# Pooled projections by seven block products, trailing sums by a scan

## The chip, the cores and the metric

The kernel runs on one core of a Trainium2 chip. The metric is the device time of one execution in microseconds (us); a time given for a kernel is the median over several executions. The core has five engines that run their own instruction queues in order and meet through semaphores: TensorE (PE, with its weight loads listed as PEld), VectorE (DVE), ScalarE (ACT), GpSimd (POOL) and SyncE (SP), which here issues DMA transfers. Matrix products read operands in SBUF, the on-chip memory of 128 partitions, and leave results in eight PSUM banks of 128 x 512 fp32.

## The reference

The model is a trunk of two residual layers on an input of 512 tokens by 1024 channels. Each layer computes x + RMSNorm(mixer(RMSNorm(x))). The first layer's mixer has mLSTM heads and stick-breaking attention and is not touched. The second layer's mixer is the one that the change concerns:

```python
def odd_layer(x, pre_g, post_g, w_in, pool_w, pool_scale, w_out):
    h = rmsnorm(x, pre_g)
    u = h @ w_in                                # (512 x 1024) @ (1024 x 4096)
    p, z = u[..., :C_WIDTH], u[..., C_WIDTH:]   # 2048 columns each
    pooled = multiscale_pool(p.reshape(Bn, S, C_GROUPS, C_GROUP_DIM))   # 4 groups of 512
    mixed = jnp.einsum('bsgc,gce->bsge', pooled, pool_w)                # one 512 x 512 map a group
    mixed = mixed.reshape(Bn, S, C_WIDTH) * pool_scale
    y = (mixed * jax.nn.silu(z)) @ w_out
    return x + rmsnorm(y, post_g)
```

`multiscale_pool` takes, for each group, the mean of the last 2, 4, 8 or 16 tokens (fewer at the start) and subtracts the token itself.

## The kernel before

All data are fp32 and every large product is made of three matmuls in a reduced-precision fp32 type. The helper `split` (lines 70 to 72) cuts an operand into a high part (a ScalarE copy, line 71) and the rest (a VectorE subtraction, line 72); `mm3` (lines 93 to 97) then adds high x high, high x low and low x high into one PSUM bank. A weight is loaded by one DMA on the SP queue into one of two 1 MB buffers (`load`, line 83), split by `halves` into one of four pairs of buffers `wh`/`wl`, and used as the stationary operand. Activations lie transposed, channels on partitions and the 512 tokens along the free axis: `hTh` and `hTl` hold the normalised input's two parts.

The second layer loops over the four groups (line 734). For each group it does the following.

- **The pooled columns p**: four chunks of 128 channels, taken as two pairs of 256 columns. Group one does them in two token halves. Groups two to four call `project2` (line 751): for each pair one load, two splits of 128 x 1024, and for each chunk 24 matmuls of 512 tokens (8 channel blocks x 3 terms) into a bank `pj`, copied out by ScalarE (line 752).
- **Pooling** (lines 753 to 775): each chunk's tile has 16 zero columns ahead of its 512 tokens. Window sums are made by doubling: 1, 2, 3 or 4 adds of a shifted copy on VectorE (line 762), each into a new tile whose leading zeros POOL sets (line 761). POOL corrects the first tokens, whose windows are shorter (lines 767 and 768), VectorE scales the sum and subtracts the token (line 769), and `split` makes the operand `pph`, `ppl`.
- **The gate columns z**: two pairs of 256 columns. In groups two to four they are made by `strassen2` (line 688), with SiLU on the way out.
- **The map** `mx`: one load and two splits of the group's 512 x 512 map `pw`, then four tiles of 12 matmuls of 512 tokens into the two banks `ac`. VectorE multiplies each tile with the scale and the gate (line 797).

`strassen2` computes a product of 256 columns by 512 tokens as a 2 x 2 block product (channel halves, column halves, token halves) with seven block products instead of eight. The token-side sums are made once, after group one, by `hidden_sums`. For each pair VectorE makes four sums of weight blocks, four split sets follow (`first` to `fourth`, the last one half as wide), and the products go in this order, each of 12 matmuls of 256 tokens:

```python
product(pa, first, 0, "11", True, True);  A.activation(t1, pa, AF.Copy)
product(pb, first, 4, "21", True, True);  V.tensor_tensor(dsts[0][:, :256], pb, t1, op=ALU.add)
product(pa, second, 0, "n2", False, True); A.activation(t2, pa, AF.Copy)
product(pe, second, 4, "d1", True, True); A.activation(t5, pe, AF.Copy)
product(pa, third, 0, "d3", False, True)
V.scalar_tensor_tensor(dsts[1][:, 256:], pa, -1.0, t5, op0=ALU.mult, op1=ALU.subtract)
product(pe, third, 4, "22", False, True); V.tensor_tensor(dsts[0][:, 256:], pe, t2, op=ALU.add)
product(pa, fourth, 0, "t4", False, True)
```

The bank `pa` is one of the two `pj`, `pb` is `xa` and `pe` is `xb`, of which there is one each. `pa` goes on accumulating after it has been read, so each later product into it must come after the read.

The order of the instructions on each engine is fixed when the kernel is built. The framework takes the program as written, estimates each instruction's time, and places each one where its engine would be free and its operands ready. On the chip the order stays as placed, so an engine whose next instruction waits does nothing else, even where another would be ready. Among the matmuls of one group's map stand some of the next group's pooled matmuls.

Of the kernel before, what the change touches and what calls it, by code (L numbers as in the profile page):

```python
# [5 lines left out]
F32 = mybir.dt.float32  # L6
F32R = mybir.dt.float32r
AF = mybir.ActivationFunctionType
ALU = mybir.AluOpType
# [4 lines left out]
P = 128  # L14
S = 512
# [21 lines left out]
def body(nc, tc, x, pre_g, post_g, w_in, conv, b_i, b_f, hn_g, w_out, w_in_c, pool_w,  # L37
         pool_scale, w_out_c, out):
    V, A, G, T = nc.vector, nc.scalar, nc.gpsimd, nc.tensor
# [4 lines left out]
    with base as base, psum as psum, dram as dram:  # L44
# [141 lines left out]
        def col_load(src, name):  # L186

            w = load(lambda t: [(nc.sync, t, src)], 8, 256, name)
            return [lambda i=i: halves(w[:, :, i * P:i * P + P], f"{name}_{i}") for i in range(2)]
# [6 lines left out]
        def project2(src, name):  # L196
            for i, w in enumerate(col_load(src, name)):
                ps = pj(f"ps_{name}_{i}")
                col_proj(w(), ps)
                yield ps  # L200

        with tc.tile_pool(name="att", bufs=1) as at:
# [25 lines left out]
            for tt in range(NB):  # L228
                prenorm(xt0[tt], xs0[tt % 2], tt, gain0, f"p0{tt}", 1 if tt else 2)
                if tt == 0:  # L230
                    for i in range(2):
                        if i:
                            nc.sync.dma_start(xt0[1], xr[:, 1])
                        w = load(lambda t: [(nc.sync, t[:, 2 * j:2 * j + 2],
                                             w_in[0, 512 * i + 256 * j:512 * i + 256 * j + 256,
                                                  VB:VB + 512]) for j in range(2)], 4, 512, f"v01{i}")
# [352 lines left out]
            for h in range(HA):  # L589
# [7 lines left out]
                for s in range(NB):  # L597
                    t = bc[:, ROW[s]:ROW[s] + P]
# [28 lines left out]
        with tc.tile_pool(name="odd", bufs=1) as od:  # L627
# [60 lines left out]
            def strassen2(src, name, dsts, silu=False):  # L688

                w = load(lambda t: [(nc.sync, t, src)], 8, 256, name)  # L690
                a11, a12, a21, a22 = (w[:, 4 * k:4 * k + 4, m * P:m * P + P]
                                      for m in range(2) for k in range(2))
                sums = [ws(f"ws{i}_{name}") for i in range(2)]
                s1, s2, s3, s4 = sums[0][:, 4:], sums[0][:, :4], sums[1][:, :4], sums[1][:, 4:]
                first = halves(w[:, :, :P], f"{name}_a")
                V.tensor_tensor(s1, a21, a22, op=ALU.add)
                V.tensor_tensor(s2, s1, a11, op=ALU.add)
                second = halves(sums[0], f"{name}_b")
                V.tensor_tensor(s3, a11, a21, op=ALU.add)
                V.tensor_tensor(s4, a12, s2, op=ALU.add)  # L700
                third = halves(sums[1], f"{name}_c")
                fourth = halves(a22, f"{name}_d")

                def product(ps, wt, k0, b, start, stop):
                    (wh, wl), (bh, bl) = wt, hs[b]
                    for k in range(4):
                        mm3(ps, (wh[:, k0 + k], wl[:, k0 + k]), (bh[:, k], bl[:, k]),
                            start and k == 0, stop and k == 3, skip_group_check=True)

                def part(i): return od.tile([P, 256], F32, tag="part", bufs=4, name=f"pt{i}_{name}")  # L710

                pa, pb, pe = (f(f"ps{n}_{name}")[:, :256] for f, n in ((pj, "a"), (xa, "b"), (xb, "e")))
                t1, t2, t5 = part(1), part(2), part(5)
                product(pa, first, 0, "11", True, True)
                A.activation(t1, pa, AF.Copy)
                product(pb, first, 4, "21", True, True)
                V.tensor_tensor(dsts[0][:, :256], pb, t1, op=ALU.add)
                product(pa, second, 0, "n2", False, True)
                A.activation(t2, pa, AF.Copy)
                product(pe, second, 4, "d1", True, True)  # L720
                A.activation(t5, pe, AF.Copy)
                product(pa, third, 0, "d3", False, True)
                V.scalar_tensor_tensor(dsts[1][:, 256:], pa, -1.0, t5, op0=ALU.mult, op1=ALU.subtract)
                product(pe, third, 4, "22", False, True)
                V.tensor_tensor(dsts[0][:, 256:], pe, t2, op=ALU.add)
                product(pa, fourth, 0, "t4", False, True)
                if silu:
                    act(dsts[0], dsts[0], AF.Silu)
                    act(dsts[1][:, 256:], dsts[1][:, 256:], AF.Silu)
                    act(dsts[1][:, :256], pa, AF.Silu, scale=-1.0)  # L730
                else:
                    A.activation(dsts[1][:, :256], pa, AF.Copy, scale=-1.0)

            for g, w in enumerate(WINDOWS):
                pooled = []
                cur4 = []
                for j in range(4):
                    c = 4 * g + j
                    cur = od.tile([P, 16 + S], F32, tag="win", bufs=6, name=f"p_{c}")
                    G.memset(cur[:, :16], 0.0)  # L740
                    cur4.append(cur)
                wsrc = [w_in_c[0, :, 512 * g + 256 * i:512 * g + 256 * i + 256] for i in range(2)]
                if g == 0:
                    wj = [t() for i in range(2) for t in col_load(wsrc[i], f"p{g}{i}")]
                    for j, n0 in ((j, n0) for n0 in (0, 256) for j in range(4)):
                        ps = pj(f"ps_p{4 * g + j}_{n0}")
                        col_proj(wj[j], ps, n0, n0 + 256)
                        A.activation(cur4[j][:, 16 + n0:16 + n0 + 256], ps[:, n0:n0 + 256], AF.Copy)  # L748
                else:
                    for i in range(2):  # L750
                        for j, ps in enumerate(project2(wsrc[i], f"p{g}{i}")):
                            A.activation(cur4[2 * i + j][:, 16:], ps, AF.Copy)
                for j in range(4):
                    c = 4 * g + j
                    cur = cur4[j]
                    p32 = cur[:, 16:]
                    sh = 1
                    while sh < w:
                        nx = od.tile([P, 16 + S], F32, tag="win", bufs=6, name=f"p_{c}_{sh}")
                        if 2 * sh < w:  # L760
                            G.memset(nx[:, :16], 0.0)
                        V.tensor_tensor(nx[:, 16:], cur[:, 16:], cur[:, 16 - sh:16 + S - sh],  # L762
                                        op=ALU.add)
                        cur, sh = nx, 2 * sh
                    sm = cur[:, 16:]
                    e = w - 1
                    G.tensor_tensor(sm[:, :e], sm[:, :e], invc[:, :e], op=ALU.mult)  # L767
                    G.tensor_tensor(sm[:, :e], sm[:, :e], p32[:, :e], op=ALU.subtract)
                    V.scalar_tensor_tensor(sm[:, e:], sm[:, e:], 1.0 / w, p32[:, e:], op0=ALU.mult,
                                           op1=ALU.subtract)  # L770
                    ph = od.tile([P, S], F32R, tag="phi", bufs=5, name=f"pph{c}")
                    pl = od.tile([P, S], F32R, tag="plo", bufs=5, name=f"ppl{c}")
                    split(sm, ph, pl)
                    pooled.append((ph, pl))
                sz = []
                for i in range(2):
                    zsrc = w_in_c[0, :, 2048 + 512 * g + 256 * i:2304 + 512 * g + 256 * i]
                    pair = [od.tile([P, S], F32, tag="sz", bufs=4, name=f"sz{4 * g + 2 * i + j}")
                            for j in range(2)]
                    if g == 0:  # L780
                        for j, ps in enumerate(project2(zsrc, f"z{g}{i}")):
                            act(pair[j], ps, AF.Silu)
                    else:
                        strassen2(zsrc, f"z{g}{i}", pair, True)
                    sz.extend(pair)
                if g == 0:
                    hidden_sums()
                w4 = load(lambda t: [(nc.sync, t, pool_w[0, g])], 4, 512, f"pw{g}")
                pw = [halves(w4[:, 2 * i:2 * i + 2], f"pw{g}{i}") for i in range(2)]
                for e in range(4):  # L790
                    c = 4 * g + e
                    ps = ac(f"mx{c}")
                    for k in range(4):
                        wh, wl = pw[k // 2]
                        mm3(ps, (wh[:, k % 2, e * P:e * P + P], wl[:, k % 2, e * P:e * P + P]),
                            pooled[k], k == 0, k == 3)
                    V.scalar_tensor_tensor(y32[:, c], ps, psc(c), sz[e], op0=ALU.mult, op1=ALU.mult)
# [44 lines left out]
```

## Time and profile before

| | before |
|---|---|
| median of 3 runs | 914.85 us (914.61 to 915.66) |
| profiled execution | 914.12 us, span 912.2 us |
| busy PE, PEld | 897.8 us, 764.9 us |
| busy DVE, ACT, POOL | 570.6, 485.6, 77.3 us |
| mean granted TensorE clock | 0.995 |
| HBM read | 96.02 MB |

The profiled execution is one run with the profiler on; its span goes from the first to the last instruction, and its own time is 1.9 us longer. A row of a group of instructions gives the line of the kernel (often a helper's line), the engine and the operation, the tiles written and read, the shape and the count; then the busy time, the mean duration of one in ns, and the idle time of the engine before them with what ended it. In a row of the timeline the first two numbers are the start and the duration in us, and square brackets hold the idle time before the instruction. A matmul's row lasts until its results are out, so rows of consecutive matmuls overlap.

### The profile page before, as it was taken

Reading aid. Unit: us, or ns where it says so; the run is one execution under the profiler, and the core shown is the slowest. Engines: PE = TensorE matmul, PEld = TensorE weight load, DVE = VectorE, ACT = ScalarE, POOL = GpSimd, SP = SyncE. Lnnn points to the kernel's source line nnn. Section 1 sums busy time; section 2 is a strip of 40 time slices with the busy share of each in tenths; the row PEclk is TensorE's granted clock in tenths of the full one; section 3 lists DMA queues with packets and bytes.
Section 4 is the critical chain, followed back from the end, with each engine's and each line's share of the span. In section 5 each row is a group of like instructions: output and inputs, shape, how many; then the busy total and the mean of one; then the engine's idle time right before and its main releaser. Section 6 shows DMA issues by size and latency. Waiting matters only on the chain.

```text
span 912.2 us, 12027 instructions
## 1 busy us (share of the span) xinstructions
PE 897.8 (98%) x4669; PEld 764.9 (84%) x4669; DVE 570.6 (63%) x847; ACT 485.6 (53%) x814; POOL 77.3 (8%) x221
## 2 busy tenths in 40 slices
PE   7999999999999999999999999999999999999996
PEld 6788889889988888898898887898889898988885
DVE  5435546567876685664775738578484867957442
ACT  6426676766668464564565527574244343455331
POOL 2001101001101201001001000005020110200000
PEclk8999999999999999999999999999999999999999
DMA  8231322222222421333312456623223233146321
GB/s 301 79 107 47 94 71 69 70 70 60 81 93 87 133 93 66 113 94 127 98 49 91 139 185 210 205 93 119 66 92 117 71 127 105 51 160 231 132 96 46
DMA packets 67128, 98.91 MB, mean 108 GB/s; under 512 B 2848, under 2 KB 54136, under 8 KB 67072
## 3 DMA queue, kind: packets, MB, share of 16 engines
q1 hardware_dynamic: 65888, 98.08, 32.7%
q8 instruction: 36, 0.59, 0.2%
q10 hardware_dynamic: 1184, 0.08, 0.1%
q14 instruction: 20, 0.16, 0.1%
HBM read 96.02 MB, written 2.13 MB: 108 GB/s over the span
## 4 chain that ended last, share of the span: by engine, by line
PE 96%; DVE 1%; ACT 1%; DMA 1%; issue 0%; SPq 0%; DVEq 0%; POOL 0%; POOLq 0%; ACTq 0%
PE op L540 10%; PE oq L540 10%; PE ps_qa L97 3%; PE ps_qa L95 3%; PE ps_qa L96 3%; PE ps_p L95 3%; PE ps_p L97 3%; PE ps_p L96 3%; PE psv_va L95 2%; PE psv_va L97 2%; PE psv_va L96 2%; PE ps_zb L95 2%; PE mx L96 2%; PE mx L97 2%; PE mx L95 2%; PE ps_oa L96 2%
## 5 line engine op out<-in xcount | busy, mean ns | idle before, releaser
L95 PE MATMUL ps_p<-hTh,wh_p 128*128 128x512 f32 (+1 forms) x160 | 55.8, 350 | 0.4 <-ACT p L748 0.4
L96 PE MATMUL ps_p<-hTl,wh_p 128*128 128x512 f32 (+1 forms) x160 | 55.9, 350 | 0.2 <-DVE hTl L72 0.2
L97 PE MATMUL ps_p<-hTh,wl_p 128*128 128x512 f32 (+1 forms) x160 | 55.7, 348 | 0.0
L97 PE MATMUL ps_qa<-hTh,wl_qa 128*128 128x512 f32 x128 | 50.3, 393 | 0.0
L95 PE MATMUL ps_qa<-hTh,wh_qa 128*128 128x512 f32 x128 | 50.2, 393 | 0.0
L96 PE MATMUL ps_qa<-hTl,wh_qa 128*128 128x512 f32 x128 | 50.2, 392 | 0.0
L72 DVE TENSOR_TENSOR wl_wo_e<-w_wo_e,wh_wo_e 128x1024 fp32r<-128x1024 f32 x28 | 34.3, 1232 | 23.3 <-ACT wh_wo_e L71 23.2
L71 ACT ACTIVATE wh_wo_e<-w_wo_e 128x1024 fp32r<-128x1024 f32 x28 | 29.4, 1058 | 29.0 <-DMA w_wo_e<-in_w_out_ab 12.3
L71 ACT ACTIVATE wh_p<-w_p 128x1024 fp32r<-128x1024 f32 x16 | 16.9, 1058 | 51.1 <-issue 31.9
L540 PE MATMUL op<-wh_wo_e,yl_e 128*128 128x512 f32 x120 | 39.1, 396 | 0.0
L540 PE MATMUL op<-wl_wo_e,yh_e 128*128 128x512 f32 x120 | 39.1, 396 | 0.0
L540 PE MATMUL op<-wh_wo_e,yh_e 128*128 128x512 f32 x120 | 37.8, 395 | 0.0
L67 ACT ACT_TABLE_LOAD x28 | 35.9, 1283 | 1.3 <-PEq L827 0.8
L97 PE MATMUL psv_va<-wh_va,hTl 128*128 128x256 f32 x128 | 36.1, 282 | 0.0
L95 PE MATMUL psv_va<-wh_va,hTh 128*128 128x256 f32 x128 | 36.1, 282 | 0.0
L96 PE MATMUL psv_va<-wl_va,hTh 128*128 128x256 f32 x128 | 36.1, 282 | 0.0
L320 DVE SCALAR_TENSOR_TENSOR cv<-u,vecs,cv 128x511 f32<-128x511 f32 (+2 forms) x48 | 35.4, 748 | 0.4
L95 PEld LDWEIGHTS ps_p<-hTh,wh_p 128*128 128x128 f32 x160 | 30.1, 189 | 4.7 <-ACT p L748 0.6
L96 PEld LDWEIGHTS ps_p<-hTl,wh_p 128*128 128x128 f32 x160 | 30.2, 189 | 4.3 <-DVE hTl L72 0.4
L97 PEld LDWEIGHTS ps_p<-hTh,wl_p 128*128 128x128 f32 x160 | 30.2, 189 | 4.1
L72 DVE TENSOR_TENSOR wl_wo_o<-w_wo_o,wh_wo_o 128x1024 fp32r<-128x1024 f32 x20 | 24.3, 1223 | 12.5 <-ACT wh_wo_o L71 12.4
L767 POOL TENSOR_TENSOR p<-p,invc 128x1 f32<-128x1 f32 (+3 forms) x16 | 18.4, 1151 | 157.8 <-DVE p L762 157.7
(379 smaller groups left out, 2826.9 us busy)
## 6 DMA issues: line engine op xcount, KB each, us to landing
w_wo_e<-in_w_out_ab SPq DMA_DIRECT2D x14, 1024.0 KB, 4.8
w_wo_o<-in_w_out_c SPq DMA_DIRECT2D x12, 1024.0 KB, 4.8
w_qa<-in_w_in_ab SPq DMA_DIRECT2D x8, 1024.0 KB, 4.9
w_p<-in_w_in_c SPq DMA_DIRECT2D x8, 1024.0 KB, 5.3
w_z<-in_w_in_c SPq DMA_DIRECT2D x8, 1024.0 KB, 5.3
w_qb<-in_w_in_ab SPq DMA_DIRECT2D x4, 1024.0 KB
w_kb<-in_w_in_ab SPq DMA_DIRECT2D x4, 1024.0 KB, 5.2
w_zb<-in_w_in_ab SPq DMA_DIRECT2D x4, 1024.0 KB, 5.1
```

Source lines behind the costliest of these rows:

```text
L67: link(A.preload_act_table_set(TABLE[func]))
L71: A.activation(hi, src, AF.Copy)
L72: V.tensor_tensor(lo, src, hi.bitcast(F32), op=ALU.subtract)
L95: T.matmul(dst, lhsT=ah, rhs=bh, start=first, stop=False, **kw)
L96: T.matmul(dst, lhsT=ah, rhs=bl, start=False, stop=False, **kw)
L97: T.matmul(dst, lhsT=al, rhs=bh, start=False, stop=last, **kw)
L320: V.scalar_tensor_tensor(acc[:, j:], u[:, :S - j], cw(3 - j, c), acc[:, j:], op0=ALU.mult, op1=ALU.add)
L540: T.matmul(ps[a][n], lhsT=l[:, ta], rhs=r[:, 0, n * 512:n * 512 + 512], start=(first and l is yh and r is wh), stop=(last and l is yl))
L767: G.tensor_tensor(sm[:, :e], sm[:, :e], invc[:, :e], op=ALU.mult)
```

## The change

Two things change in the loop over the groups. In groups two to four the two pooled pairs are made by `strassen2` in place of `project2`; its results are written straight into the chunks' tiles behind the 16 zero columns. The window sums of 4, 8 and 16 are made by one instruction for each chunk, a scan along the tokens: the running sum takes in the new token and gives up the one that leaves the window, `w` columns back, where the leading zeros stand in for tokens before the first. The window of 2 keeps its single add. Tiles for intermediate sums, and the clears of their leading columns, are gone. The gate pairs, the map, the loads and the output projection are written as before.

```diff
                 else:
                     for i in range(2):
-                        for j, ps in enumerate(project2(wsrc[i], f"p{g}{i}")):
-                            A.activation(cur4[2 * i + j][:, 16:], ps, AF.Copy)
+                        strassen2(wsrc[i], f"p{g}{i}", [t[:, 16:] for t in cur4[2 * i:2 * i + 2]])
                 for j in range(4):
                     c = 4 * g + j
                     cur = cur4[j]
                     p32 = cur[:, 16:]
-                    sh = 1
-                    while sh < w:
-                        nx = od.tile([P, 16 + S], F32, tag="win", bufs=6, name=f"p_{c}_{sh}")
-                        if 2 * sh < w:
-                            G.memset(nx[:, :16], 0.0)
-                        V.tensor_tensor(nx[:, 16:], cur[:, 16:], cur[:, 16 - sh:16 + S - sh],
-                                        op=ALU.add)
-                        cur, sh = nx, 2 * sh
-                    sm = cur[:, 16:]
+                    sm = od.tile([P, 16 + S], F32, tag="win", bufs=6, name=f"s_{c}")[:, 16:]
+                    if w == 2:
+                        V.tensor_tensor(sm, p32, cur[:, 15:15 + S], op=ALU.add)
+                    else:
+                        V.tensor_tensor_scan(sm, p32, cur[:, 16 - w:16 + S - w], 0.0, ALU.add,
+                                             ALU.subtract)
```

## The prediction

> **What bounds the kernel now.** I first read the page: its busy shares and the chain that ended last.
>
> ```profile
> span 912.2 us, 12027 instructions
> ...
> PE 897.8 (98%) x4669; PEld 764.9 (84%) x4669; DVE 570.6 (63%) x847; ACT 485.6 (53%) x814; POOL 77.3 (8%) x221
> ...
> PE 96%; DVE 1%; ACT 1%; DMA 1%; issue 0%; SPq 0%; DVEq 0%; POOL 0%; POOLq 0%; ACTq 0%
> ```
>
> TensorE (PE) is 96% of the chain, so time leaves only where TensorE's own work shrinks. Shares are averages, so I next asked for the busy time in the three stretches that hold groups two, three and four (windows of 4, 8, 16), each from one group's map matmuls `mx` to the next's. The columns are the length, then the busy time and records of PE, PEld, DVE, ACT and POOL.
>
> ```profile
> 650.00:702.70 52.70, 52.70 (x311) 46.54 (x310) 34.50 (x48) 22.35 (x34) 5.11 (x17) 1.00 0.28 89
> 702.70:756.25 53.55, 53.55 (x314) 47.26 (x313) 38.11 (x54) 21.84 (x34) 6.64 (x20) 1.00 0.31 99
> 756.25:809.60 53.35, 53.35 (x313) 46.98 (x313) 40.65 (x58) 22.68 (x35) 6.51 (x18) 1.00 0.33 109
> ```
>
> PE is busy for the whole of all three at a granted clock of 1.00. VectorE (DVE) is the next fullest, at 65 to 76%, and it is the engine onto which the change puts work.
>
> A busy PE may still hide small gaps, because one matmul lasts longer than the distance to the next start. So I take start-to-start distances. The first fence is one of the three groups of matmuls (one for each of the lines 95, 96 and 97, all of 8) in one 128-column half of a pooled pair. The second has the busy time of the gate pairs' stretch, which already uses seven products, from its first matmul to the first `mx`, and of four pooled halves.
>
> ```profile
> L95 PE MATMUL ps_p<-hTh,wh_p 128*128 128x512 f32 x8 | 3.1, 389 | 0.0
> ```
>
> ```profile
> 677.48:694.24 16.76, 16.76 (x142) 16.76 (x141) 10.90 (x16) 11.19 (x19) 1.59 (x10) 1.00 0.37 120
> ...
> 719.74:725.21 5.47, 5.47 (x26) 4.50 (x25) 4.42 (x7) 1.83 (x3) 0.24 (x2) 1.00 0.06 22
> 725.33:730.80 5.47, 5.47 (x26) 4.51 (x25) 5.26 (x9) 2.09 (x3) 1.85 (x5) 1.00 0.00 0
> 666.29:671.89 5.60, 5.60 (x27) 4.51 (x25) 4.59 (x7) 1.32 (x2) 0.11 (x1) 1.00 0.01 2
> 772.98:778.45 5.47, 5.47 (x26) 4.51 (x25) 4.93 (x8) 1.83 (x3) 1.19 (x5) 1.00 0.10 34
> ```
>
> A half is 24 matmuls (three groups of 8) in 5.47 or 5.60 us, or 0.228 to 0.233 us each. The gate stretch has 142 records, one of them running in from before: 16.76 / 141 = 0.1189 us for a 256-column matmul, with the weight loads busy throughout (16.76 of 16.76). So the seven-product form runs at the matmul pace and its weight loads don't lengthen it.
>
> **The change part by part.**
>
> *Fewer matmul columns.* A pooled pair was two halves: 2 x 5.50 (mean of the four rows) = 11.00 us, between 10.94 and 11.20. It becomes 7 products x 4 blocks x 3 terms = 84 matmuls of 256: 84 x 0.1189 = 9.99 us. A pair saves 1.01 us (0.95 to 1.21), and six pairs in three groups save **6.1 us** (5.7 to 7.3). This lies wholly on the path.
>
> *More preparation.* The durations are those of the gate pairs' same instructions, and of the old pooled split and adds, from 640 to 812 us:
>
> ```profile
> L762 DVE TENSOR_TENSOR p<-p 128x512 f32<-128x512 f32 x36 | 24.6, 686 | 1.3 <-POOL p L768 0.4
> L72 DVE TENSOR_TENSOR wl_p<-w_p,wh_p 128x1024 fp32r<-128x1024 f32 x12 | 14.7, 1221 | 11.4 <-ACT wh_p L71 11.2
> ...
> L769 DVE SCALAR_TENSOR_TENSOR p<-p,p 128x509 f32<-128x509 f32 (+2 forms) x12 | 8.2, 682 | 0.3
> ...
> L72 DVE TENSOR_TENSOR wl_z_d<-w_z,wh_z_d 128x512 fp32r<-128x512 f32 x6 | 4.1, 687 | 0.1
> ...
> L723 DVE SCALAR_TENSOR_TENSOR sz<-psa_z,pt_z 128x256 f32<-128x256 f32 x6 | 2.5, 418 | 0.0
> ```
>
> On VectorE a pair had two wide splits (2 x 1.22 = 2.44 us). It gets three wide splits and a half one (3 x 1.22 + 0.69 = 4.35), four weight sums (4 x 0.69 = 2.74, as the adds of the same shape) and three output sums (3 x 0.42 = 1.25): 8.34, which is 5.9 more per pair and 11.8 per group.
>
> *The running sum.* The 36 adds go: 8, 12 and 16 in the three groups, or 5.5, 8.2 and 11.0 us. Each of the 12 chunks gets one scan of 512 columns instead; group one keeps its add. The trace before has no scan. Its lower bound is an add, 0.686 us. A two-operation instruction (L769) costs the same 0.682, so the second operation itself is free; what is new is that each column needs the finished sum of the column before. The costliest elementwise row, in the mLSTM heads, gives the upper bound:
>
> ```profile
> L412 DVE RECIPROCAL dd<-dd 128x512 f32<-128x512 f32 x4 | 13.4, 3354 | 2.1 <-ACT dd L68 2.1
> ```
>
> The range is 0.69 to 3.35 us. I take 1.22, the row of 1024 columns, as if each column passed twice: of the three rows it is the nearest to a column that does one more round. A group's VectorE work then changes by 11.8 + 4.9 less its adds: 34.5 becomes 45.7, 38.1 becomes 46.6, 40.65 becomes 46.4 us, against TensorE stretches of 50.7, 51.5 and 51.3 (each 2 x 1.01 shorter). It is hidden by TensorE's own matmuls and costs nothing, but at 90% instead of 71% the cover is thin; without it I price it under the third rival. [...]
>
> POOL loses 24 clears of intermediate tiles, all off the chain.
>
> *What waits anew.* The split weights rotate through four buffers. A pooled pair used two, now it uses four, so its third and fourth sets inherit the buffers of the previous group's map weights and wait for the end of `mx`. The trace before shows this wait for its second pair:
>
> ```profile
> 712.44 1.22 DVE L72 TENSOR_TENSOR wl_p<-w_p,wh_p 128x1024 fp32r<-128x1024 f32 x1
> 712.50 0.39 PE L97 MATMUL mx<-pph,wl_pw 128*128 128x512 f32 x1
> ...
> 713.03 1.06 ACT L71 ACTIVATE wh_p<-w_p 128x1024 fp32r<-128x1024 f32 x1 [0.63 <-PE mx L97]
> ```
>
> The third set would be whole at 712.44 + 1.22 = 713.66, and the last `mx` gives way at 712.50 + 0.23 = 712.73: 0.9 us are to be covered. The pair's first two sets hold 48 matmuls, 48 x 0.1189 = 5.7 us. Of pooled matmuls TensorE used some as filler between the `mx` tiles:
>
> ```profile
> 702.71 0.39 PE L95 MATMUL ps_p<-hTh,wh_p 128*128 128x512 f32 x1
> ...
> 707.13 0.40 PE L95 MATMUL mx<-pph,wh_pw 128*128 128x512 f32 x1
> ```
>
> If these 4.4 us of filler stay, 1.3 us remain after `mx`, against the 0.9 needed: covered, barely. If not, up to one ScalarE and one VectorE pass (1.06 + 1.22 = 2.3 us) opens per group. Queued behind the waiting ScalarE copy are the PSUM copies of the same pair. ScalarE itself has room: a pair gives it eight instructions where it had four, none longer than this 1.06, so at most 4.2 us more a pair, or 8.5 a group on 22 of 53 us.
>
> The 1 MB weight loads keep their number and queue (SP). Their buffer frees at a pair's last split, so the first gate load now waits for the first pair's fourth set, whose copy can't start before 713.03. By the row below it lands some 5 us after that split, near 721; it is needed two pairs (20 us) after `mx`, near 732, so nothing is late.
>
> ```profile
> w_z<-in_w_in_c SPq DMA_DIRECT2D x6, 1024.0 KB, 5.3
> ```
>
> *Hand-overs between pairs.* The gate pairs follow each other with hardly a gap; the worst is in group four:
>
> ```profile
> 789.85 0.28 PE L96 MATMUL psb_z<-hTl,wh_z_a 128*128 128x256 f32 x1
> 790.05 0.38 PE L97 MATMUL psa_z<-hTh,wl_z_a 128*128 128x256 f32 x1
> ```
>
> There 0.20 us lie between starts where 0.12 is usual. A group gets two more seven-product pairs, and I charge 0.1 us, rounded up from this 0.08, for each: **0.6 us** (0 to 7, the bound being the 2.3 us per group).
>
> *The sum.* The profiled execution took 914.12 us, its span 912.2 and 1.9 around it. 914.12 - 6.1 + 0.6 = 908.6. The median of the runs is 914.85, 0.73 above, so the same change gives **909.3** there.
>
> **The rivals.**
>
> *Hand-overs eat the gain (914.1).* Inside a pair the last product accumulates into a bank that VectorE must first have read (L723). The cover is one product, 12 x 0.1189 = 1.43 us. If a scan (1.22) and a half split (0.69) stand ahead of that read (0.42), 2.33 - 1.43 = 0.9 us is lost in each of six pairs, 5.4 of the 6.1. For it: VectorE serves its queue in order and is 90% full. Against it stands a stretch of group four with two pooled halves and most of the gate pairs:
>
> ```profile
> 774.20:797.90 23.70, 23.70 (x160) 21.76 (x159) 23.10 (x35) 11.51 (x20) 5.34 (x14) 1.00 0.14 46
> ```
>
> VectorE was 97% busy, and TensorE showed no idle time beside the short gap above.
>
> *POOL is locked out (911.4).* POOL's edge correction waits while VectorE works back to back:
>
> ```profile
> 619.85 7.45 POOL L767 TENSOR_TENSOR p<-p,invc 128x1 f32<-128x1 f32 x1 [71.84 <-DVE p L762]
> ...
> 793.08 0.64 POOL L767 TENSOR_TENSOR p<-p,invc 128x15 f32<-128x15 f32 x1 [5.37 <-DVE p L762]
> 795.70 0.69 DVE L72 TENSOR_TENSOR ppl<-p,pph 128x512 fp32r<-128x512 f32 x1
> 801.10 0.39 PE L95 MATMUL mx<-pph,wh_pw 128*128 128x512 f32 x1
> ```
>
> One column took 7.45 us instead of 0.64. Were the last chunk of group four held so, 6.8 us more, it would pass its 4.7 us of slack (796.39 to 801.10) by 2.1 us. Against it: VectorE's own next step waits for POOL and so stops. [...]
>
> *VectorE becomes the bound: slower (919.4).* Here the mechanism is the scan alone. The group is VectorE-bound at its old length when 38.1 + 11.8 - 8.2 + 4X = 53.55, so X = 2.96 us; the other two groups give 2.98. At the upper bound of 3.35 the groups last 54.2, 55.1 and 54.9, together 4.6 us more than now. For it only the reciprocal's row speaks; against it, an add and subtract in one pass cost 0.68. [...]
>
> **How the numbers follow.** Forecast 0.60 at 909.3 (own range 907.5 to 911.5: 914.85 - 7.3 without a stall, and 914.85 - 5.7 with one of 2.3). POOL 0.05 at 911.4. Hand-overs 0.24 around 914.1, spread over faster 0.06, same 0.13 and slower 0.05. Scan 0.11 at 919.4. A measurement here tells 0.2%, about 1.8 us, from no change. Faster: 0.60 + 0.05 + 0.06 = 0.71; same 0.13; slower 0.05 + 0.11 = 0.16. The range runs from 907.0, the forecast's own low end less half the 1.05 us by which the three runs differ, to 915.5, which leaves out the scan's case and the dear end of the hand-overs.
>
> **What would show it.** Right: the three groups shorten to about 51.5 us with PE busy throughout; 84 matmuls of 256 per pooled pair at 0.119; the scan's row near 1.2 us; VectorE near 46 us per group. Wrong: PE idle before the pooled products of the third set or before the last product of a pair, released by VectorE or ScalarE; `mx` waiting for `ppl`; a scan row above 2.9 us; a 256-column pitch above 0.131 (11.00 / 84), at which the pairs save nothing.

## The result and the profile after

The changed kernel takes **908.97 us** (median of 6 runs, 907.92 to 910.40) against 914.66 us for the kernel before on the same chip (6 runs). The ratio is 0.9939, with a 95% interval of 0.9928 to 0.9949. A second set of five runs on another occasion gave 908.57 us and 0.9938 (0.9925 to 0.9950). The prediction was 909.3 us, within 907.0 to 915.5. The profiled execution took 910.17 us, 1.2 above the median.

The page of the changed kernel, with its busy shares and the chain that ended last:

```profile
span 908.5 us, 12491 instructions
...
PE 893.6 (98%) x4885; PEld 771.9 (85%) x4885; DVE 590.8 (65%) x877; ACT 497.9 (55%) x838; POOL 82.4 (9%) x197
...
PE 93%; DVE 3%; DMA 2%; ACT 1%; issue 1%; SPq 0%; DVEq 0%; POOL 0%; ACTq 0%; POOLq 0%
```

TensorE has 216 more matmuls and is still 98% busy, but VectorE and a DMA now hold 5% of the chain; before, they held 2%. The busy times of the three groups, each cut at its first pooled matmul and the last at the first of the output projection, show where. First the kernel before, then the changed one:

```profile
649.40:702.71 53.31, 53.31 (x314) 47.05 (x313) 34.91 (x48) 22.35 (x34) 5.11 (x17) 1.00 0.29 92
702.71:756.09 53.38, 53.38 (x314) 47.10 (x313) 37.94 (x54) 21.84 (x34) 6.64 (x20) 1.00 0.31 99
756.09:809.51 53.42, 53.42 (x314) 47.06 (x312) 40.77 (x58) 22.59 (x35) 6.51 (x18) 1.00 0.33 109
```

```profile
650.61:701.72 51.11, 51.11 (x385) 48.93 (x384) 41.05 (x58) 26.09 (x42) 7.70 (x12) 1.00 0.32 104
701.72:754.76 53.04, 51.78 (x385) 49.13 (x384) 45.23 (x63) 25.90 (x43) 7.66 (x12) 1.00 0.32 100
754.76:806.05 51.29, 51.29 (x385) 48.99 (x384) 42.81 (x59) 25.95 (x42) 7.99 (x8) 1.00 0.34 114
```

Groups two and four shortened by 2.2 and 2.1 us with PE busy throughout, group three by 0.3. Group three shows 51.78 us of busy PE in 53.04: it lost 1.3 us to waits, and more if the short gaps hidden under a matmul's own duration are counted. The view of who waited for whom on PE, from 615 to 812 us, names the two longest:

```profile
PE psa_z L97 <- DVE wl_z_a L72: 0.7, 1, 0.7
PE psa_z L95 <- DVE sz L723: 0.5, 1, 0.5
```

The first is followed in the timelines of VectorE and PE:

```profile
717.54 0.69 DVE L696 TENSOR_TENSOR ws_z<-w_z 128x512 f32<-128x512 f32 x1 [2.13 <-DMA w_z<-in_w_in_c]
...
721.07 1.21 DVE L760 TENSOR_TENSOR_SCAN s<-p 128x512 f32<-128x512 f32 x1
722.21 1.20 DVE L72 TENSOR_TENSOR wl_p_c<-ws_p,wh_p_c 128x1024 fp32r<-128x1024 f32 x1
723.32 0.68 DVE L72 TENSOR_TENSOR wl_p_d<-w_p,wh_p_d 128x512 fp32r<-128x512 f32 x1
723.93 0.68 DVE L765 SCALAR_TENSOR_TENSOR s<-s,p 128x505 f32<-128x505 f32 x1
724.53 1.21 DVE L72 TENSOR_TENSOR wl_z_a<-w_z,wh_z_a 128x1024 fp32r<-128x1024 f32 x1
```

```profile
724.79 0.27 PE L97 MATMUL psa_p<-d3h,wl_p_c 128*128 128x256 f32 x1
725.80 0.39 PE L97 MATMUL psa_z<-hTh,wl_z_a 128*128 128x256 f32 x1 [0.73 <-DVE wl_z_a L72]
```

VectorE first waited 2.13 us for the gate weights to land. Then it worked without a break, with a scan, a scaling and two other splits ahead of the split `wl_z_a`, which ended at 725.74; PE, which would have gone on at 724.91, started at 725.80. A scan's row is in the groups of lines, from 640 to 812 us:

```profile
L760 DVE TENSOR_TENSOR_SCAN s<-p 128x512 f32<-128x512 f32 x12 | 14.6, 1219 | 0.0
```

### The profile page after: what moved, and what is told of

It is laid out like the page before. It is cut to its first block, busy times and chain, and to the rows that moved or that the text cites. A ratio compares the mean times of both kernels' runs of the same rounds, so it can differ in the third digit from the quotient of the medians.

```text
span 908.5 us, 12491 instructions
## 1 busy us (share of the span) xinstructions
PE 893.6 (98%) x4885; PEld 771.9 (85%) x4885; DVE 590.8 (65%) x877; ACT 497.9 (55%) x838; POOL 82.4 (9%) x197
## 3 DMA queue, kind: packets, MB, share of 16 engines
HBM read 96.02 MB, written 2.13 MB: 108 GB/s over the span
## 4 chain that ended last, share of the span: by engine, by line
PE 93%; DVE 3%; DMA 2%; ACT 1%; issue 1%; SPq 0%; DVEq 0%; POOL 0%; ACTq 0%; POOLq 0%
PE op L540 10%; PE oq L540 10%; PE ps_qa L97 3%; PE ps_qa L96 3%; PE ps_qa L95 3%; PE psv_va L97 2%; PE psv_va L95 2%; PE psv_va L96 2%; PE ps_zb L95 2%; PE ps_oa L96 2%; PE ps_oa L97 2%; PE ps_zb L97 2%; PE ps_za L95 2%; PE ps_oa L95 2%; PE ps_qb L97 2%; PE ps_za L97 2%
## 5 line engine op out<-in xcount | busy, mean ns | idle before, releaser
L763 POOL TENSOR_TENSOR s<-s,invc 128x1 f32<-128x1 f32 (+3 forms) x16 | 19.3, 1207 | 195.4 <-DVE s L760 91.2
L72 DVE TENSOR_TENSOR wl_wo_o<-w_wo_o,wh_wo_o 128x1024 fp32r<-128x1024 f32 x20 | 24.2, 1224 | 12.2 <-ACT wh_wo_o L71 12.2
L72 DVE TENSOR_TENSOR wl_qa<-w_qa,wh_qa 128x1024 fp32r<-128x1024 f32 x16 | 19.6, 1222 | 18.4 <-ACT wh_qa L71 18.4
L540 PE MATMUL oq<-wh_wo_o,yl_o 128*128 128x512 f32 x96 | 30.7, 395 | 0.0
L540 PE MATMUL oq<-wl_wo_o,yh_o 128*128 128x512 f32 x96 | 30.4, 395 | 0.0
L540 PE MATMUL oq<-wh_wo_o,yh_o 128*128 128x512 f32 x96 | 29.7, 396 | 0.0
L71 ACT ACTIVATE wh_wo_o<-w_wo_o 128x1024 fp32r<-128x1024 f32 x20 | 20.8, 1054 | 15.4 <-PE oq L540 7.3
L96 PEld LDWEIGHTS ps_qa<-hTl,wh_qa 128*128 128x128 f32 x128 | 24.1, 188 | 5.2
L95 PEld LDWEIGHTS ps_qa<-hTh,wh_qa 128*128 128x128 f32 x128 | 24.1, 188 | 5.2
```

What stands on the lines that cost most here:

```text
L71: A.activation(hi, src, AF.Copy)
L72: V.tensor_tensor(lo, src, hi.bitcast(F32), op=ALU.subtract)
L95: T.matmul(dst, lhsT=ah, rhs=bh, start=first, stop=False, **kw)
L96: T.matmul(dst, lhsT=ah, rhs=bl, start=False, stop=False, **kw)
L540: T.matmul(ps[a][n], lhsT=l[:, ta], rhs=r[:, 0, n * 512:n * 512 + 512], start=(first and l is yh and r is wh), stop=(last and l is yl))
```

## The experiments

To compare them I measure two things in each profile. **Idle** is TensorE's idle time from 640 to 830 us: where the distance between two matmul starts exceeds the usual (0.2335 us for 512 columns, 0.12 for 256) by over 0.05 us, the excess is summed. **Tail** is the time from the start of the longest unbroken run of matmuls of the first layer's output projection (185 of them, as the chain lists them) to the end of the span. That start is 504.51 us in the kernel before and 505.72 in the changed one, and in the profiles of the table it lies between 502.45 and 505.79: the beginning, which nobody changed, varies, and the tail leaves that out.

```profile
504.51 43.15 PE op L540 x185
```

```profile
505.72 43.15 PE op L540 x185
```

So the tail is 912.2 - 504.51 = 407.69 us before and 908.5 - 505.72 = 402.78 us after.

| kernel | median us | ratio to before (95%) | tail | idle | tail less idle |
|---|---|---|---|---|---|
| before | 914.66 | | 407.69 | 0.19 | 407.50 |
| changed | 908.97 | 0.9939 (0.9928-0.9949) | 402.78 | 2.06 | 400.72 |
| after_again | 908.57 | 0.9938 (0.9925-0.9950) | 401.98 | 1.35 | 400.63 |
| e1_products | 917.81 | 1.0040 (1.0026-1.0055) | 409.95 | 9.10 | 400.85 |
| e2_scan | 914.40 | 0.9998 (0.9989-1.0007) | 407.91 | 0.50 | 407.41 |
| e3_add | 907.80 | 0.9929 (0.9915-0.9943) | 401.16 | 0.47 | 400.69 |
| e4_scan3 | 921.57 | 1.0082 (1.0069-1.0094) | 414.49 | 13.86 | 400.63 |
| e5_order | 907.55 | 0.9924 (0.9912-0.9937) | 401.43 | 0.54 | 400.89 |
| e7_pool | 911.99 | 0.9966 (0.9952-0.9979) | 406.16 | 5.54 | 400.62 |
| e8_scan16 | 908.27 | 0.9930 (0.9918-0.9943) | 402.17 | 1.47 | 400.70 |
| e10_load | 909.83 | 0.9949 (0.9934-0.9963) | 403.87 | 2.96 | 400.91 |
| e11_queue | 912.73 | 0.9983 (0.9970-0.9995) | 405.75 | 4.91 | 400.84 |
| e12_five | 912.80 | 0.9991 (0.9977-1.0006) | 405.86 | 5.13 | 400.73 |

The last column is the main finding. Every kernel with the seven products has 400.6 to 400.9 us, and the two without have 407.4 and 407.5. The products save 407.46 - 400.75 = 6.7 us of matmul time (means of the two and of the eleven) whatever surrounds them; all other differences of the tails are idle TensorE.

### The two parts alone, and the price of the scan

**e1_products** puts the doubling adds back:

```diff
-                    sm = od.tile([P, 16 + S], F32, tag="win", bufs=6, name=f"s_{c}")[:, 16:]
...
-                        V.tensor_tensor_scan(sm, p32, cur[:, 16 - w:16 + S - w], 0.0, ALU.add,
-                                             ALU.subtract)
+                    sh = 1
+                    while sh < w:
+                        nx = od.tile([P, 16 + S], F32, tag="win", bufs=6, name=f"p_{c}_{sh}")
...
+                        cur, sh = nx, 2 * sh
+                    sm = cur[:, 16:]
```

> The seven products alone; the window sums are made by doubling adds as before. The changed kernel (908.97 us) has 1.9 us of idle TensorE in its third group and 0.2 in the fourth. Theory A, VectorE's queue: the seven products save 6 to 7 us of matmul time, and what is lost is TensorE waiting for a VectorE that is behind with its queue. Without the scan VectorE has 0.6, 3.3 and 6.1 us more to do in groups two, three and four (adds 5.5, 8.2, 11.0 for scans of 4.9), so more is lost: 910 to 913 us, with the idle time of TensorE in groups three and four above 3 us. Theory B, the pairs' own hand-overs or the later gate load: what is lost does not depend on VectorE's load, so 908.5 to 909.5 us with the same idle places.

Measured: 917.81 us, **slower than the kernel before**, and outside what either theory expected. Theory B falls: what is lost is not fixed by the pairs' own hand-overs. Theory A named the side but not the size. TensorE's longest wait is not for a split or a bank, but for a pooled chunk in group four:

```profile
PE mx L95 <- ACT pph L71: 6.0, 2, 5.1
```

VectorE's 36 doubling adds, from 640 to 812 us, have no idle time in front of them, so on the chip none of them waited for a free tile or for POOL's clears:

```profile
L761 DVE TENSOR_TENSOR p<-p 128x512 f32<-128x512 f32 x36 | 24.3, 683 | 0.0
```

**e2_scan** puts `project2` back and keeps the scan:

```diff
-                        strassen2(wsrc[i], f"p{g}{i}", [t[:, 16:] for t in cur4[2 * i:2 * i + 2]])
+                        for j, ps in enumerate(project2(wsrc[i], f"p{g}{i}")):
+                            A.activation(cur4[2 * i + j][:, 16:], ps, AF.Copy)
```

> The scan alone; the pooled pairs are made by the plain products as before. Theory A: TensorE was busy throughout in these groups, so VectorE's relief (0.6, 3.3, 6.1 us a group) brings nothing: 914.0 to 915.3 us. Theory B expects the same. A third view, that the scan shortens a chain that TensorE waits for, would give 912 to 913.5 us.

Measured: 914.40 us, ratio 0.9998. Alone the scan does nothing. So the parts don't add up: +0.4% and nothing make -0.6% together.

**e3_add** replaces each scan by one add, so it leaves the sums of 4, 8 and 16 tokens out:

```diff
-                        V.tensor_tensor_scan(sm, p32, cur[:, 16 - w:16 + S - w], 0.0, ALU.add,
-                                             ALU.subtract)
+                        V.tensor_tensor(sm, p32, cur[:, 16 - w:16 + S - w], op=ALU.add)
```

> The changed kernel with each of the twelve scans replaced by one plain add of the same shape, so that the window sums of 4, 8 and 16 tokens are left out and each holds two terms only. VectorE has 12 x 0.53 = 6.4 us less to do. Theory A: the idle 1.9 us of group three shrink to under 0.7, so 907.0 to 908.0 us. Theory B: 908.5 to 909.5 us with the same idle places.

Measured: 907.80 us with 0.47 us idle. Every engine executes its instructions in the same order as in the changed kernel, so nothing differs but how long these twelve take. As theory A expected, VectorE's queue holds most of the changed kernel's lost microsecond, and theory B's fixed hand-overs are not seen. The late gate load is not ruled out by this run; see after_again.

**e4_scan3** makes each scan three times:

```diff
+                        for _ in range(3):
                             V.tensor_tensor_scan(sm, p32, cur[:, 16 - w:16 + S - w], 0.0,
                                                  ALU.add, ALU.subtract)
```

> The changed kernel with each scan made three times into the same tile: VectorE gets 2 x 4 x 1.22 = 9.8 us more a group, which stands for a scan of 3.66 us, above the 2.96 us from which the prediction called the group VectorE-bound. By measured VectorE work (41.1, 45.2, 42.8 us) the groups would hold 50.9, 55.0 and 52.6 us of it. Theory A: groups three and four become VectorE-bound, 913 to 919 us. Theory B: VectorE still has room in its own gaps, 909 to 911 us.

Measured: 921.57 us, 6.9 above the kernel before (914.70 in that set) and above what theory A expected; idle TensorE appears in all three groups. The waits on PE:

```profile
PE psa_z L97 <- DVE wl_z_a L72: 4.9, 3, 1.7
PE mx L97 <- DVE wl_pw L72: 1.5, 3, 0.6
PE pse_z L95 <- DVE p L725: 1.2, 2, 0.6
PE psa_p L95 <- DVE p L723: 1.1, 1, 1.1
```

These four are the longest, all for VectorE's splits or PSUM reads; beside them stand 0.9 us for a chunk's split on ScalarE and 0.3 for another read. VectorE is busy 52.5 of 55.0 us in group three and 53.7 of 56.5 in group four, so these two are VectorE-bound; in group two, which also lost time, it is busy 46.8 of 54.9. The slower rival's sum for a scan of 3.66 us gives groups of 55.4, 56.4 and 56.1 us, 8.3 more than before, against the 6.9 measured.

### What the order of VectorE's queue is worth

**after_again** is the changed kernel, beside the next three.

> The changed kernel itself, beside the next three on one chip: both theories 908.3 to 909.7 us.

Measured: 908.57 us with 1.35 us idle in its profile, against 2.06 in the first. The program is the same, and the waits of group three differ: only the bank read shows, 0.4 us, and no wait for `wl_z_a`. The gate weights had landed earlier:

```profile
714.82 0.69 DVE L696 TENSOR_TENSOR ws_z<-w_z 128x512 f32<-128x512 f32 x1 [0.92 <-DMA w_z<-in_w_in_c]
```

From the projection's start that is 714.82 - 504.22 = 210.60 us, against 717.54 - 505.72 = 211.82 in the first profile. So the longest gap of the first profile took both: work ahead of the split and a load that came 1.2 us later. In e3_add the load came at 210.96, so that run alone does not separate the two; what it takes from after_again's 1.35 us of idle time, to 0.47, is the scans'.

**e5_order** moves the scans behind the gate splits. The pooling is written after the gate pairs, and each scan gets an order-only condition. With that the planner also placed TensorE's and ScalarE's instructions in another order from group two on:

```diff
+                            sn = V.tensor_tensor_scan(sm, p32, cur[:, 16 - w:16 + S - w], 0.0,
+                                                      ALU.add, ALU.subtract)
+                            tc.add_manual_dep(sn.ins, marks[j].ins.name, NOSYNC, reason="queue order")
```

where `marks` are the first two weight splits of each gate pair.

> The changed kernel with nothing but VectorE's order changed: by an order-only dependency each chunk's scan stands behind a weight split of the gate pairs (chunks 0 and 1 behind the first two splits of the first gate pair, 2 and 3 behind those of the second). The work is the same. Theory A, VectorE's queue: TensorE waited in group three for the split wl_z_a (0.7 us) and a bank read (0.5), which stood behind scans; the gaps go and the kernel takes 907.0 to 908.3 us, near the kernel with cheap adds in place of scans (907.80). Theory B, the late gate load: 908.5 to 909.5 us, the same gaps. A third way: the pooled chunks now come too late for the map, and the kernel takes over 910 us.

Measured: 907.55 us (907.38 to 908.13, five runs), within theory A's range. Its VectorE timeline in group three has the split 4.9 us after the gate weights landed, where the first profile has 7.0, with the scan behind it:

```profile
716.09 0.69 DVE L698 TENSOR_TENSOR ws_z<-w_z 128x512 f32<-128x512 f32 x1 [1.11 <-DMA w_z<-in_w_in_c]
...
720.43 0.68 DVE L74 TENSOR_TENSOR wl_p_d<-w_p,wh_p_d 128x512 fp32r<-128x512 f32 x1
721.03 1.22 DVE L74 TENSOR_TENSOR wl_z_a<-w_z,wh_z_a 128x1024 fp32r<-128x1024 f32 x1
722.17 1.21 DVE L766 TENSOR_TENSOR_SCAN s<-p 128x512 f32<-128x512 f32 x1
```

TensorE's idle time fell to 0.54 us with the work unchanged. Its median is the lowest of the table; against the changed kernel beside it (907.92 to 909.97) the gain is 1.0 us, and the two intervals of the ratios overlap. Since more than VectorE's order changed, this run supports theory A and does not prove it alone.

**e7_pool** gives one of four weight sums to POOL:

```diff
-                V.tensor_tensor(s3, a11, a21, op=ALU.add)
+                G.tensor_tensor(s3, a11, a21, op=ALU.add)
```

> The changed kernel with one of the four weight sums of each seven-product pair (the sum of the two blocks of the first column half) made on POOL in place of VectorE: 0.69 us less for VectorE in each of twelve pairs. Theory A: less backlog, 907.3 to 908.5 us. [...]

Measured: 911.99 us, 3.4 slower than the changed kernel and 3.5 above theory A's range. The moved sum and the sum that VectorE makes of the same load, from 640 to 812 us:

```profile
L699 POOL TENSOR_TENSOR ws_z<-w_z 128x512 f32<-128x512 f32 x6 | 10.0, 1664 | 46.9 <-DMA w_z<-in_w_in_c 46.9
```

```profile
L696 DVE TENSOR_TENSOR ws_z<-w_z 128x512 f32<-128x512 f32 x6 | 7.4, 1235 | 3.1 <-DMA w_z<-in_w_in_c 3.1
```

VectorE's own sum grew from 690 ns in the changed kernel to 1235. POOL took 1.66 us for what costs VectorE 0.68, and in these gate pairs 0.55 of the 0.68 us of relief was lost again. TensorE's longest waits are for bank reads in VectorE's queue:

```profile
PE psb_z L95 <- DVE sz L717: 1.2, 3, 0.4
PE psb_z L95 <- DVE p L717: 1.1, 1, 1.1
```

### Why the products alone are slow

**e8_scan16** keeps the products and uses the scan in group four only:

```diff
+                    if w == 16:
+                        sm = od.tile([P, 16 + S], F32, tag="win", bufs=6, name=f"s_{c}")[:, 16:]
...
+                    else:
+                        sh = 1
+                        while sh < w:
...
```

> Seven products in groups two to four as in the changed kernel, the scan in group four (window 16) only, doubling adds for windows of 4 and 8. The products alone took 917.81 us, with 1.2 us of idle TensorE in group three and 7.7 in group four. Theory A, VectorE's load group by group: the adds of group four (11.0 us for 4.9 of scans) carry that loss; without them 909 to 911 us. If instead the loss of the products alone comes from the order that the planner happens to choose, or from the adds of all groups, it stays above 913 us.

Measured: 908.27 us, as fast as the changed kernel. The whole loss of the products alone sits in group four, and four scans remove it. But VectorE's load (theory L below) is only one thing that they change there: four serial adds pass through several tiles, the scan needs one.

**e10_load** keeps the scan and adds load: one dummy add ahead of each scan in group three, two in group four.

```diff
+                        for _ in range(WINDOWS.index(w) - 1):
+                            V.tensor_tensor(sm, p32, cur[:, 16 - w:16 + S - w], op=ALU.add)
                         V.tensor_tensor_scan(sm, p32, cur[:, 16 - w:16 + S - w], 0.0, ALU.add,
                                              ALU.subtract)
```

> The changed kernel with one extra add of 512 columns before each scan in group three and two in group four, written into the tile that the scan then overwrites; nothing is left out. VectorE's work is about that of the doubling adds (1.9 and 2.6 us a chunk for 2.1 and 2.7), with one tile for each chunk as with the scan. Theory L, VectorE's load made the products alone slow (917.81): 914 to 918 us, group four losing 5 us or more. Theory S, the shape of the doubling: serial adds that pass through few tiles, and what the planner put ahead of the late chunks: 908.5 to 911.5 us.

Measured: 909.83 us with 2.96 us idle. Theory L falls: nearly the same VectorE work as in e1_products costs about 1 us, not 9. What is left is the shape of the doubling and the order that the planner made of it.

**e11_queue** is e1_products with a condition on ScalarE's order: the output projection's first weight splits stand behind the split of group four's last chunk.

```diff
+            if last.get("hold"):
+                tc.add_manual_dep(i.ins, last["high"].ins.name, NOSYNC, reason="queue order")
```

> The seven products alone with doubling adds (917.81 us), with one more condition on the order: the output projection's first weight splits on ScalarE stand behind the split of group four's last pooled chunk (order only, no work changed). Before, two of them stood ahead of the last two chunks on ScalarE and VectorE, and ScalarE waited 4.0 us for their weights to land while TensorE waited 5.2 us for a pooled chunk. Theory S with the queue as its cause: 911 to 914 us. Theory L: the chunks are late by VectorE's load, and 915.5 to 918 us remain.

Measured: 912.73 us, 5.1 less than e1_products. In e1_products ScalarE's timeline shows what stood in the way:

```profile
801.50 2.00 ACT L71 ACTIVATE wh_wo_o<-w_wo_o 128x1024 fp32r<-128x1024 f32 x2 [4.02 <-DMA w_wo_o<-in_w_out_c]
803.41 0.92 ACT L68 ACTIVATE sz<-sz 128x512 f32<-128x512 f32 x2
804.24 0.36 ACT L68 ACTIVATE sz<-psa_z 128x256 f32<-128x256 f32 x1
804.62 1.28 ACT L67 ACT_TABLE_LOAD   x1
805.91 0.63 ACT L71 ACTIVATE pph<-p 128x512 fp32r<-128x512 f32 x1
```

The pooled chunk's split (`pph`) stood behind two splits of output weights that had not landed, and behind three SiLU passes and a table load that they held up. TensorE waited from 801.4 to 806.6 us for it. With the order turned round, the longest such wait is 1.5 us:

```profile
PE mx L100 <- ACT pph L73: 2.6, 2, 1.5
```

**e12_five** is the changed kernel with `bufs=5` in place of `bufs=6` for the chunks and their sums.

```diff
-tag="win", bufs=6
+tag="win", bufs=5
```

> The changed kernel with five tiles in place of six for the chunks and their sums: four hold the group's chunks, so one is left for a sum, and a chunk's scan waits until the chunk before it is split or a chunk's tile is free. The work is the same. Theory S, few tiles serialise the chunks and make them late: 911 us or more, TensorE waiting for a pooled chunk. Theory L: 908.3 to 909.7 us.

Measured: 912.80 us with 5.13 us idle. The time is what theory S expected, the place is not: no matmul of the map waited for a chunk. The waits on PE are for a PSUM copy and for splits:

```profile
PE psa_z L95 <- ACT pt_z L715: 1.6, 1, 1.6
PE psa_z L97 <- DVE wl_z_c L72: 1.1, 2, 0.7
```

and ScalarE's timeline shows the copy behind a late chunk's split that had held the queue for 4.65 us:

```profile
740.51 0.63 ACT L71 ACTIVATE pph<-s 128x512 fp32r<-128x512 f32 x1 [4.65 <-POOL p L740]
741.05 1.04 ACT L71 ACTIVATE wh_z_c<-ws_z 128x1024 fp32r<-128x1024 f32 x1
741.99 0.36 ACT L715 ACTIVATE pt_z<-psa_z 128x256 f32<-128x256 f32 x1
```

That chunk was late on POOL, which corrects its first seven columns:

```profile
726.71 0.58 POOL L763 TENSOR_TENSOR s<-s,invc 128x7 f32<-128x7 f32 x1 [3.21 <-DVE s L760]
...
734.26 5.04 POOL L763 TENSOR_TENSOR s<-s,invc 128x7 f32<-128x7 f32 x1 [5.84 <-DVE s L760]
```

The same correction took 0.58 us for the chunk before and 5.04 for this one, while VectorE worked without a break from 732.90 to 740.75. The other wait, for `wl_z_c`, is for a split directly behind a scan, much as in the changed kernel. VectorE idled 0.2 us in all before its twelve scans, so they did not wait for tiles. That few tiles make chunks late is therefore not shown: a late chunk in an in-order queue delays other work of TensorE, and here POOL made it late. How the 9.1 us of e1_products divide beyond the 4 to 5 that the queue order explains (4.2 of idle time in the profiles, 5.1 between the medians) stays open between the order that few tiles and serial adds led the planner to, POOL's corrections and load.

## Why the prediction was right, point by point

**The matmul saving** was put at 6.1 us (5.7 to 7.3). The runs show 6.7 us, 1.12 a pair. The mechanism was right and the term a little small. The 256-column matmul was dear by a trace: in group four of the changed kernel one row covers 265 of them, 31.54 us less 0.18 of gaps, or 0.1183 us each against 0.1189, which is 0.05 us a pair.

```profile
766.06:797.60 31.54, 31.54 (x266) 31.42 (x265) 30.04 (x43) 19.93 (x33) 7.99 (x8) 1.00 0.36 116
```

The rest lies with the pooled pair: 84 x 0.1183 + 1.12 = 11.06 us, where I had averaged four of twelve halves to 11.00.

**The charge for hand-overs** was 0.6 us, with ends of 0 and 7. The two profiles show 2.06 and 1.35 us idle, 0.19 of which was there before, so 1.2 to 1.9 us. This term was too small by two or three times. With the saving too small as well, the two errors nearly cancel: 6.7 less 1.2 to 1.9 is 4.8 to 5.5 us, 5.5 was forecast, and the medians differ by 5.7. That the forecast came within 0.4 us is in part luck.

**VectorE's load** was put at 45.7, 46.6 and 46.4 us a group and was 41.1, 45.2 and 42.8. The prediction added 25.4 us of durations for the three groups, and VectorE's durations, summed over the span, did grow by 25.5. Its busy time grew by 590.8 - 570.6 = 20.2 only: rows of VectorE that follow each other overlap by 0.07 to 0.09 us (the scan at 721.07 lasts 1.21 us, the next row starts at 722.21), which adding durations leaves out. The price of the scan, 1.22 us, an estimate taken from the row of 1024 columns, was right to the last figure (1219 ns). But the claim that this work "is hidden by TensorE's own matmuls and costs nothing" was wrong in group three: with cheap adds the kernel gains 0.8 us on one set of runs of the changed kernel and 1.2 on the other (e3_add). It was hidden on average, and not in its place in the queue.

**The new wait at the start of a pair**, for the map's weight buffers, was "covered, barely". It was covered: neither profile has a gap there. The planner kept pooled matmuls as filler between the map's tiles.

**The moved gate load** was to land near 721, needed near 732, "so nothing is late". It landed by 717.54, but the planner had put the first gate matmuls into the pooled pair as filler, at 723.00 already, and VectorE idled 2.13 us for the load just ahead of the stretch in which it fell behind:

```profile
723.00 0.28 PE L95 MATMUL psb_z<-hTh,wh_z_a 128*128 128x256 f32 x1
```

This is the step that the prediction had wrong: I took the gate pair to start where the pooled pair ends. The trace before already shows otherwise, with gate matmuls among the pooled ones from 719.49 us on.

**The rivals.** *Hand-overs*: its mechanism, a bank read behind a scan, took 0.5 us once in the first profile, in a gate pair, not 0.9 in each of six pairs. *POOL locked out*: no wait of the map's matmuls for a chunk is seen in the changed kernel, but a slow correction is. In group four one of fifteen columns took 3.42 us, while VectorE had no idle time from 784.10 to 792.37, against a mean of 0.54 for the three other chunks; there was time to spare:

```profile
785.69 3.42 POOL L764 TENSOR_TENSOR s<-s,p 128x15 f32<-128x15 f32 x1
```

In e12_five one of 5.04 us did reach TensorE, by way of ScalarE's queue and not of the map. *VectorE as the bound*: it does not occur, since the scan takes 1.22 us; at three times that it does, and its sum (8.3 us) is near what was measured (6.9). By the traces a scan of 512 columns took 1219 ns and an add 686.

**What the prediction did not see** is that the second part carries the first. By its load sums the products with doubling adds would fill VectorE in group four with 40.65 + 11.8 = 52.5 us, 1.1 over TensorE's 51.3, so about 910 us; they took 917.8, with VectorE busy 50.5 of that group's 59.4 us. What the scan brings is not mainly VectorE time (e10_load). A better order behind it is shown for 4 to 5 us (e11_queue); that this comes of one tile and one step for each chunk is likely and not shown.

## What to carry to other kernels

A change that takes matmul time out of a TensorE-bound stretch can hand part of it back as waits for the engines that feed it, here 1.2 to 1.9 of 6.7 us; so price both, and price the second by the order of the queues, not by the busy share. When TensorE waits for an engine that is only 85% busy, look in that engine's timeline for work without a deadline that stands ahead of the work waited for; an order-only dependency that turns the two round adds no work, and here the kernel with it was 1.0 us faster (e5_order). An engine that is hardly busy can matter too: one correction of 5.04 us on POOL held ScalarE's queue for 4.65 us (e12_five). Time each part of a change alone before judging it: here one part alone is slower than nothing, the other does nothing, and the two together are the gain.

## What the runs showed of the hardware

In the changed kernel a running sum over 512 fp32 columns took VectorE 1219 ns (1211 to 1226 over the twelve, with windows of 4, 8 and 16 tokens), as much as a subtraction over 1024 columns in the same stretch (means of 1212 to 1224 ns). In e7_pool, where POOL adds 128 x 512 in 1664 ns on average, VectorE's add of the same shape from the same load took 1235 ns, against 690 in the changed kernel; no run shows POOL's add alone. In e12_five a POOL instruction on 7 columns took 5.04 us, against 0.58 for the chunk before, while VectorE worked without a break.
